# Windowed attention of the odd layer: values become the stationary operand, and the softmax sums are divided inside the transposes of the probabilities

## The chip, the cores and the metric

The kernel runs on one core of a Trainium2 chip. The metric is the device time of one execution in microseconds (us). The engines are named as the profile names them: PE is TensorE's matmuls and PEld its weight loads, DVE is VectorE, ACT is ScalarE, POOL is GpSimd, SP issues most of the DMAs.

## What is computed

The program is a two-layer backbone over 256 context tokens and 512 latent tokens of width 1024. The even layer mixes mLSTM heads with differential attention, the odd layer is sliding-window attention, and each layer ends in a large expert retrieval (PEER). The change touches only the odd layer's attention. It has 16 query heads of width 64 on 4 key-value heads; each block of 128 latent queries sees the 256 context keys and the latent blocks next to it, and one sink logit per head joins the softmax:

```python
def _sink_softmax(s, sink):
    sk = jnp.broadcast_to(sink[None, :, :, None, None], s.shape[:-1] + (1,))
    p = jax.nn.softmax(jnp.concatenate([s, sk], axis=-1), axis=-1)
    return p[..., :-1]
...
        p = _sink_softmax(jnp.concatenate([s_ctx, s_loc], axis=-1), sink).astype(vi.dtype)
        return (jnp.einsum('bhgqk,bkhd->bqhgd', p[..., :tc], vc)
                + jnp.einsum('bhgqk,bkhd->bqhgd', p[..., tc:], vi))
...
    yl = _window_attend(ql, kl, vl, kc, vc, sink) @ w_out
```

## The kernel before

The odd layer's attention works in 64 units. A unit is one head and one block `b` of 128 queries; units run over two passes `p` (blocks 0 and 1, then 2 and 3), in a pass over eight head pairs `j`, and for each pair over two blocks and the two heads `hf` of the pair. Four units share one query projection (`proj`, L251, tile `oqps`).

For one unit, `odd_front` (L1294) makes the scores in PSUM (`ops`: a one-column matmul for the sink, then matmuls over 256 context columns and over 256 or 384 latent columns, then the mask matmuls), takes the row minimum on DVE (`mx`, L1313; scores are kept negated) and the exponentials on ACT (`op`, L1315), whose sum over the row goes to a column of the tile `Z` (`oz`). `odd_back` (L1318) cuts the probabilities into chunks of 128 keys: 4 for the outer blocks 0 and 3, 5 for blocks 1 and 2, 288 over all units. PE transposes each chunk against the identity (`opt`, L1329), in two groups (2+2 or 3+2); ACT copies each group out of PSUM (`opT`, L1330). Then PE multiplies the transposed chunks, as stationary operand, with the values (`oo`, L1335), and ACT copies 64 columns of the result into the token-major tile `ys[b]` (`oy`, L1337).

After the last unit, DVE takes the reciprocal of `Z` (L1287) and multiplies each block's `ys[b]` by it (L1290); PE transposes each block in 8 pieces (`xpose`, L388, tile `xps`), ACT copies it to `xt` (L390), and `out_proj` (L836) multiplies `xt` with the output weights (L223, tile `ops`, the same name as the scores).

Two other streams share this stretch. The first is what is left of the expert gather of layer 0: 64 rows fetched by POOL and added up on DVE (`pacc<-uv`, L1036), after which latent block 3 can be normalized. The second is `mod_rows` (L323): 32 weight tiles `wraw` are read by DMA and added up on DVE (`macc`, L332 and L334) for layer 1's modulation rows. They share a ring of three `wraw` buffers with the weights of the projections.

The order of the instructions on each engine is fixed when the kernel is built, by a scheduler that weighs priorities and estimated times; on the chip each engine works through its own list and waits where it must. PSUM tiles of the kinds `opt`, `oo` and `rps` share two buffers, score tiles another two.

Of the kernel before, what the change touches and what calls it, by code (L numbers as in the profile page):

```python
# [9 lines left out]
F32 = mybir.dt.float32  # L10
# [3 lines left out]
AF = mybir.ActivationFunctionType  # L14
OP = mybir.AluOpType
AX = mybir.AxisListType

D = 1024
# [92 lines left out]
class Kern:  # L111
# [1071 lines left out]
    def odd(self, xs, tok_lat, late):  # L1183
        nc, a = self.nc, self.a
        wn = self.wk

        def norm_blocks(blocks, xt):
            old, self.wk = self.wk, wn
            self.norm_blocks(1, LAT, tok_lat, blocks, xt)
            self.wk = old  # L1190

        w_in = "od_w_in"
        xtc = self.xt_tiles(256)
        for b in range(2):
            self.xpose(xs[b], xtc, b)
        with self.tc.tile_pool(name="odk", bufs=1, reuse_waits="tile") as pk:
            KT = [[pk.tile([128, 768], F32R, name="okt%s%d" % (x, j)) for x in "hl"] for j in range(2)]
            V = pk.tile([128, 6, 256], F32, name="ov")

            snk = pk.tile([128, 16], BF16, name="snk")  # L1200
            rest = pk.tile([128, 16], F32, name="snr")
            part = pk.tile([128, 16], BF16, name="snp")
            nc.sync.dma_start(rest, a["od_sink"].broadcast_to([128, 16]))
            nc.gpsimd.memset(snk, 0.0)
            nc.vector.tensor_scalar(rest, rest, -1.0, None, op0=OP.mult)
            for r in range(3):
                nc.vector.tensor_copy(part, rest)
                nc.vector.scalar_tensor_tensor(snk, part, self.ident[:, r:r + 1], snk, op0=OP.mult, op1=OP.add)
                if r < 2:
                    nc.vector.tensor_tensor(rest, rest, part, op=OP.subtract)  # L1210
            bfc = pk.tile([128, 4, 128], BF16, name="bfc")
            for i, n in enumerate(("ident", "mf", "mb", "ones")):
                nc.vector.tensor_scalar(bfc[:, i, :], self.c(n), -1.0 if n in ("mf", "mb") else 1.0, None,
                                        op0=OP.mult)
            def keys(xt, c0, T, lat, skip=0):

                for j in range(2):
                    ps = self.pj([128, T], "okps")
                    self.projT(ps, self.wT(w_in, 1024 + 128 * j), xt, T, c0)
                    n = T - skip  # L1220
                    k = ps[:, skip:T]
                    if lat:
                        r = self.t2k([128, n], "okr")
                        self.rope(k, n, [(r, slice(0, 128))], c0 + skip)
                        k = r
                    hi, lo = (t[:, 256 * lat + c0 + skip:256 * lat + c0 + T] for t in KT[j])
                    nc.scalar.copy(hi, k)
                    nc.vector.tensor_tensor(lo, k, hi.bitcast(F32), op=OP.subtract)

            def values(xt, blocks, lat):  # L1230
                wv = [self.wN(w_in, 1280, h) for h in range(2)]
                for b in blocks:
                    ps = self.pj([128, 256], "vps")
                    self.projN(ps, wv, xt, b)
                    nc.scalar.copy(V[:, 2 * lat + b, :], ps)

            with self.later():
                late()
            with self.phase("okv"):
                keys(xtc, 0, 256, 0)  # L1240
                values(xtc, range(2), 0)
            xt = self.xt_tiles(512)
            norm_blocks(range(3), xt)
            with self.phase("okv"):
                keys(xt, 0, 384, 1)
                values(xt, range(3), 1)
            with self.phase("oat"):
                ys = [self.wk.tile([128, D], F32, name="oy%d" % b) for b in range(4)]
                Z = self.wk.tile([128, 4, 16], F32, name="oz")

                def proj(p, j):
                    ps = self.pj([128, 256], "oqps")
                    self.projT(ps, self.wT(w_in, 128 * j), xt, 256, 256 * p)
                    r = self.t2k([128, 256], "oqr")
                    self.rope(ps, 256, [(r, slice(0, 128))], 256 * p, -(64.0 ** -0.5))
                    t = [self.wk.tile([128, 2, 256], F32R, name="oq" + x, tag="oq" + x, bufs=2) for x in "hl"]
                    for n, ps in enumerate((slice(0, 64), slice(64, 128))):
                        hi, lo = t[0][ps, n, :], t[1][ps, n, :]
                        nc.scalar.copy(hi, r[ps, :])
                        nc.vector.tensor_tensor(lo, r[ps, :], hi.bitcast(F32), op=OP.subtract)  # L1260
                        for x in t:
                            nc.gpsimd.memset(x[ps, 1 - n, :].bitcast(F32), 0.0)
                    return t

                units = [(j, b, hf) for p in range(2) for j in range(8)
                         for b in (2 * p, 2 * p + 1) for hf in range(2)]
                qs = {(0, 0): proj(0, 0)}
                mods = self.mod_rows(1, [2, 4, 3, 5])

                def front(u):  # L1270
                    j, b, hf = u
                    p = b // 2
                    if MS == 0 and hf or MS == 1 and p == 1 or MS == 2 and (p == 1 or hf and j >= 4):
                        next(mods, None)
                    if b % 2 == 1 and hf == 0:
                        if (p, j) == (0, 7):
                            norm_blocks([3], xt)
                            keys(xt, 256, 256, 1, 128)
                            values(xt, [3], 1)
                        if (p, j) != (1, 7):  # L1280
                            nx = (p, j + 1) if j < 7 else (1, 0)
                            qs[nx] = proj(*nx)
                    return self.odd_front(j, b, hf, qs[p, j], KT[j // 4], snk, bfc, Z)

                self.pipe(units, front, lambda u, r: self.odd_back(*u, r, V, ys))
                xt = self.xt_tiles(512)
                nc.vector.reciprocal(Z, Z)  # L1287
                for b in range(4):
                    y = ys[b].rearrange("p (h d) -> p h d", h=16)
                    nc.vector.tensor_tensor(y, y, Z[:, b, :].unsqueeze(2).broadcast_to([128, 16, 64]), op=OP.mult)  # L1290
                    self.xpose(ys[b], xt, b)
        return xt

    def odd_front(self, j, b, hf, qp, kt, snk, bfc, Z):  # L1294
        nc, wk = self.nc, self.wk
        h = 8 * (j // 4) + 4 * hf + j % 4
        lo, hi = max(b - 1, 0), min(b + 1, 3)
        n = 128 * (hi - lo + 1)
# [4 lines left out]
        for c, d, m in ((0, 256, 256), (256 + 128 * lo, 512, n)):  # L1303
            for i, (x, y) in enumerate(((0, 0), (0, 1), (1, 0))):
                nc.tensor.matmul(S[:, d:d + m], q[x], kt[y][:, c:c + m], start=(i == 0),
                                 stop=(i == 2 and d == 256))
        masks = ([(0, 1)] if lo < b else []) + ([(n - 128, 2)] if hi > b else [])
        for i, (o, m) in enumerate(masks):
            nc.tensor.matmul(S[:, 512 + o:640 + o], bfc[:, 0, :], bfc[:, m, :], start=False,
                             stop=(i == len(masks) - 1))  # L1310
# [1 line left out]
        mx = wk.tile([128, 1], F32, name="mx", tag="mx", bufs=4)  # L1312
        nc.vector.tensor_reduce(mx, Sv, axis=AX.X, op=OP.min)  # L1313
        p = wk.tile([128, 641], F32, name="op", tag="op", bufs=3)
        nc.scalar.activation(p[:, 0:257 + n], Sv, AF.Exp, bias=mx, scale=-1.0, accum_out=Z[:, b, h:h + 1])  # L1315
        return p

    def odd_back(self, j, b, hf, p, V, ys):  # L1318
        nc, wk = self.nc, self.wk
        h = 8 * (j // 4) + 4 * hf + j % 4  # L1320
        lo, hi = max(b - 1, 0), min(b + 1, 3)
        kb = 2 + hi - lo + 1
        pT = wk.tile([128, kb, 128], F32, name="opT", tag="opT", bufs=2)
        i0 = 0
        for n in ((2, 2) if kb == 4 else (3, 2)):
            pt = self.po([128, n, 128], "opt")
            for i in range(n):
                c = 1 + 128 * (i0 + i)
                nc.tensor.transpose(pt[:, i, :], p[:, c:c + 128], self.ident)  # L1329
            nc.scalar.copy(pT[:, i0:i0 + n, :], pt)  # L1330
            i0 += n
        po = self.po([128, 128], "oo")
        for i in range(kb):
            vb = i if i < 2 else 2 + lo + i - 2
            nc.tensor.matmul(po, pT[:, i, :], V[:, vb, 128 * (j // 4):128 * (j // 4) + 128],  # L1335
                             start=(i == 0), stop=(i == kb - 1))
        nc.scalar.copy(ys[b][:, 64 * h:64 * h + 64], po[:, 64 * hf:64 * hf + 64])  # L1337


    def peer(self, l, xt, bb, gat, rows, done, late, put):  # L1340
# [134 lines left out]
def layout(i):  # L1475
# [26 lines left out]
        heads += [8 * (j // 4) + j % 4, 8 * (j // 4) + 4 + j % 4]  # L1502
    cols = np.concatenate([np.arange(64 * h, 64 * h + 64) for h in heads])
    ws["od_w_in"] = np.concatenate([w[:, cols], w[:, 1024:]], 1)
    ws["od_w_out"] = f("od_w_out")[0]
    o["od_sink"] = f("od_sink")
    for l in range(2):
        ws["pr_w_q%d" % l] = f("pr_w_q")[l]
# [8 lines left out]
    u = f("pr_u")  # L1517
# [30 lines left out]
```

## Time and profile before

| what | value |
|---|---|
| time, median of 3 runs | 4202.02 us (4199.56 to 4206.68) |
| the profiled execution | 4207.51 us, of which the span is 4205.7 us |
| PE / PEld busy | 3816.9 us (91%) / 3259.6 us (78%) |
| DVE busy | 3316.6 us (79%) |
| ACT / POOL busy | 1508.1 us (36%) / 2261.8 us (54%) |
| mean granted TensorE clock | 0.955 of full speed |

The span is the time from the first to the last instruction; the profiled execution's own time is 1.8 us longer. Busy shares are means over stages with different limits: the odd layer's attention fills about 290 us from 2490 us to 2782 us of the span, and it has to be read there.

### The profile page before, as it was taken

The numbers are of one execution on the slowest core, as the hardware profiler recorded it, in microseconds if no ns is written. First come the engines' busy times: TensorE is split into PE (matmuls) and PEld (weight loads), VectorE is DVE, ScalarE is ACT, GpSimd is POOL, SyncE is SP. The second block draws the span as 40 slices with busy tenths as digits, with TensorE's granted clock in tenths as the row PEclk, the third lists the DMA queues.
The fourth block names the chain that finished last, engine by engine and source line by source line (L and its number), as shares of the span: only waits on it lengthen the run. The fifth ranks groups of instructions, "written<-read, shape, count | busy, mean of one in ns | idle before, by whom it ended". The sixth has DMA issues, their size and how long they took to land.

```text
span 4205.7 us, 56328 instructions
## 1 busy us (share of the span) xinstructions
PE 3816.9 (91%) x19774; PEld 3259.6 (78%) x19780; DVE 3316.6 (79%) x5835; ACT 1508.1 (36%) x2746; POOL 2261.8 (54%) x1644
## 2 busy tenths in 40 slices
PE   8988776769888799999999889999989999999999
PEld 5776554547777699988999767777877899999987
DVE  4359888866998899989999987537875977777788
ACT  3322322312146333333333324332356333333333
POOL 1016777542454587877888563004531666666664
PEclk9999888879999999999999999999999999999999
DMA  5556898783449999999999995423346988787878
GB/s 192 172 200 209 308 322 307 253 287 121 149 161 398 367 332 334 332 324 333 346 339 331 341 333 194 158 85 111 111 160 235 346 279 285 275 290 273 282 268 313
DMA packets 389674, 1099.30 MB, mean 261 GB/s; under 512 B 32959, under 2 KB 140807, under 8 KB 383246
## 3 DMA queue, kind: packets, MB, share of 16 engines
q0 software_dynamic: 147456, 536.94, 35.2%
q1 hardware_dynamic: 232142, 497.95, 34.6%
q10 hardware_dynamic: 9792, 60.82, 3.5%
q8 instruction: 155, 2.54, 0.2%
q14 instruction: 129, 1.06, 0.1%
HBM read 1024.18 MB, written 71.40 MB: 260 GB/s over the span
## 4 chain that ended last, share of the span: by engine, by line
PE 58%; DVE 16%; DMA 11%; issue 8%; POOL 6%; ACT 2%; SPq 0%; ACTq 0%; POOLq 0%; DVEq 0%
PE dacc L1178 20%; PE dA L217 18%; POOL uv L1010 4%; DMA uv<-in_pr_u_dram,ix 3%; PE ops L223 3%; DMA uv<-in_pr_v_dram,ix 3%; PE pqps L217 2%; DVE junkv L1023 2%; PE gps L1108 2%; DMA draw<-in_uT_dram 1%; PE oo L1335 1%; DVE pacc L1036 1%; PE gds L1091 1%; PE modps L252 1%; PE oqps L210 1%
## 5 line engine op out<-in xcount | busy, mean ns | idle before, releaser
L1178 PE MATMUL dacc<-dhi,dw 128*128 128x512 f32 x3072 | 983.7, 390 | 3.4 <-ACT dw L1171 1.9
L1010 POOL DMA_INDIRECT uv<-in_pr_u_dram,ix x512 | 669.4, 1307 | 447.7 <-DVE pa L1023 316.0
L1010 POOL DMA_INDIRECT uv<-in_pr_v_dram,ix x512 | 680.0, 1328 | 408.0 <-DVE pacc L1036 281.9
L1023 DVE CUSTOM_DVE_ANT_0 junkv<-uv,x 128x1024 bf16<-128x1024 f32 x512 | 692.6, 1353 | 65.0 <-DMA uv<-in_pr_u_dram,ix 60.9
L1036 DVE SCALAR_TENSOR_TENSOR pacc<-uv,pw,pacc 128x1024 f32<-128x1024 f32 x508 | 701.5, 1381 | 39.3 <-DMA uv<-in_pr_v_dram,ix 35.4
L1178 PEld LDWEIGHTS dacc<-dhi,dw 128*128 128x128 f32 x3072 | 576.5, 188 | 119.5 <-ACT dw L1171 2.2
L1123 POOL TENSOR_TENSOR dlo<-draw,dhi 128x1024 fp32r<-128x1024 f32 x210 | 545.0, 2596 | 194.9 <-ACT dhi L1122 191.4
L1122 ACT CAST dhi<-draw 128x1024 fp32r<-128x1024 f32 x467 | 489.0, 1050 | 404.9 <-issue 179.5
L1178 PE MATMUL dacc<-dlo,dw 128*128 128x512 f32 x1536 | 601.6, 392 | 5.2 <-DVE dlo L1123 5.2
L1168 DVE TENSOR_TENSOR dz<-dz,dG 128x384 f32<-128x384 f32 x256 | 416.9, 1642 | 73.6 <-ACT dz L1138 71.8
L1171 ACT CAST dw<-dz 128x384 fp32r<-128x384 f32 x256 | 131.5, 514 | 721.2 <-PE dacc L1178 694.3
L1123 DVE TENSOR_TENSOR dlo<-draw,dhi 128x1024 fp32r<-128x1024 f32 x257 | 331.9, 1292 | 17.7 <-ACT dhi L1122 16.1
L217 PE MATMUL dA<-xth,dlo 128*128 128x384 f32 x1688 | 328.1, 335 | 19.0 <-POOL dlo L1123 19.0
L217 PE MATMUL dA<-xth,dhi 128*128 128x384 f32 x1688 | 334.6, 340 | 5.1 <-ACT dhi L1122 5.1
L1178 PEld LDWEIGHTS dacc<-dlo,dw 128*128 128x128 f32 x1536 | 288.2, 188 | 63.8 <-DVE dlo L1123 7.6
L217 PE MATMUL dA<-xtl,dhi 128*128 128x384 f32 x1688 | 326.9, 334 | 0.0
L217 PEld LDWEIGHTS dA<-xth,dhi 128*128 128x128 f32 x1688 | 305.7, 189 | 21.6 <-ACT dhi L1122 5.5
L217 PEld LDWEIGHTS dA<-xth,dlo 128*128 128x128 f32 x1688 | 296.5, 188 | 20.0 <-POOL dlo L1123 20.0
L217 PEld LDWEIGHTS dA<-xtl,dhi 128*128 128x128 f32 x1688 | 296.4, 188 | 0.0
L1172 DVE TENSOR_TENSOR dw<-dz,dw 128x384 fp32r<-128x384 f32 x256 | 154.4, 603 | 150.3 <-ACT dw L1171 150.3
L196 POOL TENSOR_TENSOR wlo<-wraw,whi 128x1024 fp32r<-128x1024 f32 x55 | 132.8, 2416 | 246.7 <-ACT whi L195 129.6
L1108 PEld LDWEIGHTS gps<-ghot 128*128 128x128 f32 x1536 | 205.0, 195 | 70.7 <-issue 39.0
(339 smaller groups left out, 6072.2 us busy)
## 6 DMA issues: line engine op xcount, KB each, us to landing
draw<-in_pr_v_dram SPq DMA_DIRECT2D x256, 512.0 KB
draw<-in_uT_dram SPq DMA_DIRECT2D x211, 512.0 KB
wraw<-in_wb_dram SPq DMA_DIRECT2D x150, 512.0 KB
gd<-gch ACTq DMA_DIRECT2D x48, 1024.0 KB
dG<-gd SPq DMA_DIRECT2D x30, 1536.0 KB
wraw<-in_mod_t_dram SPq DMA_DIRECT2D x48, 512.0 KB
wraw<-in_uT_dram SPq DMA_DIRECT2D x45, 512.0 KB
wraw<-in_mod_w_dram SPq DMA_DIRECT2D x32, 512.0 KB
```

What stands on the lines that cost most here:

```text
L196: eng.tensor_tensor(lo, raw, hi.bitcast(F32), op=OP.subtract)
L217: self.nc.tensor.matmul(ps, w[wi][:, k, :], x[xi][:, k, 0:T], start=(i == 0), stop=(i == 23))
L1010: nc.gpsimd.indirect_dma_start(out=t, out_offset=None, in_=a[table], in_offset=bass.IndirectOffsetOnAxis(ap=ix[:, c:c + 1], axis=0))
L1023: nc.vector.tensor_tensor_reduce(out=junk, in0=u, in1=x, op0=OP.mult, op1=OP.add, scale=1.0, scalar=0.0, accum_out=A[:, c:c + 1])
L1036: nc.vector.scalar_tensor_tensor(acc, v, W[:, c:c + 1], acc, op0=OP.mult, op1=OP.add)
L1108: nc.tensor.matmul(ps[0][:, t0 % 8 + t, :], h[0][:, t, :], h[1][:, t, :], start=True, stop=True)
L1122: nc.scalar.copy(hi, raw)
L1123: eng.tensor_tensor(lo, raw, hi.bitcast(F32), op=OP.subtract)
L1168: nc.vector.tensor_tensor(z3, z3, self.G[:, :, j % JG, :], op=OP.mult)
L1171: nc.scalar.copy(wh, z)
L1172: i = nc.vector.tensor_tensor(wl, z, wh.bitcast(F32), op=OP.subtract)
L1178: self.nc.tensor.matmul(acc[b][:, h, :], w[wi][:, 128 * b:128 * b + 128], v[vi][:, 512 * h:512 * h + 512], start=(j == 0 and i == 0), stop ...
```

## The change

The change turns the last product round: the values are now the stationary operand and the transposed probabilities the moving one, so `oo` comes out with the head's width on the partitions and the tokens along the row. ACT copies 64 partitions of 128 tokens straight into `yT` (tile `oy`, now allocated where the low parts of other transposed inputs lie), which is what the output projection reads. `ys`, the division at the end, the 32 transposes of `xpose` and their four copies are gone. The softmax sum must then be divided earlier: each unit takes the reciprocal of its own sum `z`, DVE multiplies the identity by it (`orz`, a 128x128 diagonal), and the transposes of the probabilities become ordinary f32 matmuls against this diagonal. The rows of the output weights are put in the order of the heads on the host.

```diff
@@ odd, phase "oat"
-                ys = [self.wk.tile([128, D], F32, name="oy%d" % b) for b in range(4)]
-                Z = self.wk.tile([128, 4, 16], F32, name="oz")
+                yT = self.px.tile([128, 8, 512], F32, name="oy", tag="xl")
...
-                    return self.odd_front(j, b, hf, qs[p, j], KT[j // 4], snk, bfc, Z)
-
-                self.pipe(units, front, lambda u, r: self.odd_back(*u, r, V, ys))
-                xt = self.xt_tiles(512)
-                nc.vector.reciprocal(Z, Z)
-                for b in range(4):
-                    y = ys[b].rearrange("p (h d) -> p h d", h=16)
-                    nc.vector.tensor_tensor(y, y, Z[:, b, :].unsqueeze(2).broadcast_to([128, 16, 64]), op=OP.mult)
-                    self.xpose(ys[b], xt, b)
+                    return self.odd_front(j, b, hf, qs[p, j], KT[j // 4], snk, bfc)
+
+                self.pipe(units, front, lambda u, r: self.odd_back(*u, r, V, yT))
+                xt = yT
         return xt
@@ odd_front
-        nc.scalar.activation(p[:, 0:257 + n], Sv, AF.Exp, bias=mx, scale=-1.0, accum_out=Z[:, b, h:h + 1])
-        return p
+        z = wk.tile([128, 1], F32, name="oz", tag="oz", bufs=4)
+        nc.scalar.activation(p[:, 0:257 + n], Sv, AF.Exp, bias=mx, scale=-1.0, accum_out=z)
+
+        nc.vector.reciprocal(z, z)
+        rz = wk.tile([128, 128], F32, name="orz", tag="orz", bufs=3)
+        nc.vector.tensor_scalar(rz, self.ident, z, None, op0=OP.mult)
+        return p, rz
@@ odd_back
-                nc.tensor.transpose(pt[:, i, :], p[:, c:c + 128], self.ident)
+                nc.tensor.matmul(pt[:, i, :], p[:, c:c + 128], rz, start=True, stop=True)
...
-            nc.tensor.matmul(po, pT[:, i, :], V[:, vb, 128 * (j // 4):128 * (j // 4) + 128],
+            nc.tensor.matmul(po, V[:, vb, 128 * (j // 4):128 * (j // 4) + 128], pT[:, i, :],
                              start=(i == 0), stop=(i == kb - 1))
-        nc.scalar.copy(ys[b][:, 64 * h:64 * h + 64], po[:, 64 * hf:64 * hf + 64])
+        rows = slice(64 * hf, 64 * hf + 64)
+        nc.scalar.copy(yT[rows, j, 128 * b:128 * b + 128], po[rows, :])
@@ layout, on the host
-    ws["od_w_out"] = f("od_w_out")[0]
+    ws["od_w_out"] = f("od_w_out")[0][cols]
```

The first place is the end of the attention on PE. Before, between the last units and the output projection (`oo` are value products, `opt` transposes of probabilities, `xps` transposes of finished blocks, `ops<-wraw,xt` the output projection):

```order
L388 MATMUL xps<-cst,oy_19361 128x128 x8
L1335 MATMUL oo<-ov,opT 128x128 x2
L388 MATMUL xps<-cst,oy_19362 128x128 x8
L223 MATMUL ops<-wraw,xt 128x256 x5
L1335 MATMUL oo<-ov,opT 128x128 x2
L1329 MATMUL opt<-cst,op 128x128 x2
L223 MATMUL ops<-wraw,xt 128x256 x10
L1329 MATMUL opt<-cst,op 128x128 x2
L1335 MATMUL oo<-ov,opT 128x128 x2
L223 MATMUL ops<-wraw,xt 128x256
L1335 MATMUL oo<-ov,opT 128x128 x2
L388 MATMUL xps<-cst,oy_19363 128x128 x8
```

In the changed kernel, the same place up to the output projection (`ops<-wraw,oy`):

```order
L1329 MATMUL opt<-orz,op 128x128 x5
L1335 MATMUL oo<-opT,ov 128x128 x5
L1329 MATMUL opt<-orz,op 128x128 x5
L1335 MATMUL oo<-opT,ov 128x128 x5
L1329 MATMUL opt<-orz,op 128x128 x4
L1335 MATMUL oo<-opT,ov 128x128 x4
L1329 MATMUL opt<-orz,op 128x128 x4
L1335 MATMUL oo<-opT,ov 128x128 x4
L223 MATMUL ops<-wraw,oy 128x256 x112
L388 MATMUL xps<-cst,xn 128x128 x32
```

The groups of `xps` (three of the four show here) are gone, and the output projection, of which 16 matmuls stood between the last units, now begins after the last of them.

The second place is DVE in the stretch where the expert gather is still being added up (`pacc`); before, for the second group of four units:

```order
L1313 TENSOR_REDUCE mx<-ops 128x1 x2
L1036 SCALAR_TENSOR_TENSOR pacc<-uv,pw,pacc 128x1024
L334 SCALAR_TENSOR_TENSOR macc<-wraw,sc,macc 128x1024
L1036 SCALAR_TENSOR_TENSOR pacc<-uv,pw,pacc 128x1024
L1313 TENSOR_REDUCE mx<-ops 128x1
L334 SCALAR_TENSOR_TENSOR macc<-wraw,sc,macc 128x1024
L1313 TENSOR_REDUCE mx<-ops 128x1
L1036 SCALAR_TENSOR_TENSOR pacc<-uv,pw,pacc 128x1024
L725 TENSOR_TENSOR rt_19600<-rps,cst 128x256
L726 TENSOR_TENSOR rraw<-rraw,cst 128x256
```

In the changed kernel, for the same four units:

```order
L1307 TENSOR_REDUCE mx<-ops 128x1
L1312 RECIPROCAL oz<-oz 128x1
L334 SCALAR_TENSOR_TENSOR macc<-wraw,sc,macc 128x1024
L1314 TENSOR_SCALAR orz<-cst,oz 128x128
L1307 TENSOR_REDUCE mx<-ops 128x1
L1036 SCALAR_TENSOR_TENSOR pacc<-uv,pw,pacc 128x1024
L1312 RECIPROCAL oz<-oz 128x1
L1307 TENSOR_REDUCE mx<-ops 128x1
L1036 SCALAR_TENSOR_TENSOR pacc<-uv,pw,pacc 128x1024
L334 SCALAR_TENSOR_TENSOR macc<-wraw,sc,macc 128x1024
L1314 TENSOR_SCALAR orz<-cst,oz 128x128
L1312 RECIPROCAL oz<-oz 128x1
```

Each unit adds one RECIPROCAL (`oz`) and one TENSOR_SCALAR (`orz`), set between the sums of the gather and of the modulation rows.

The third place is PE in the second pass, where nothing but attention is left. Before, between the scores of two blocks:

```order
L1335 MATMUL oo<-ov,opT 128x128 x4
L1329 MATMUL opt<-cst,op 128x128 x2
L1302 LDWEIGHTS bfc
L1302 MATMUL ops<-snk,bfc 128x1
L1305 MATMUL ops<-okth_18937,oqh 128x256
L1305 MATMUL ops<-oktl_18938,oqh 128x256
L1305 MATMUL ops<-okth_18937,oql 128x256
L1305 MATMUL ops<-okth_18937,oqh 128x256
L1305 MATMUL ops<-oktl_18938,oqh 128x256
L1305 MATMUL ops<-okth_18937,oql 128x256
```

In the changed kernel:

```order
L1329 MATMUL opt<-orz,op 128x128 x2
L1335 MATMUL oo<-opT,ov 128x128 x2
L1296 LDWEIGHTS bfc
L1296 MATMUL ops<-snk,bfc 128x1
L1299 MATMUL ops<-okth_18937,oqh 128x256
L1299 MATMUL ops<-oktl_18938,oqh 128x256
L1299 MATMUL ops<-okth_18937,oql 128x256
L1299 MATMUL ops<-okth_18937,oqh 128x256
L1299 MATMUL ops<-oktl_18938,oqh 128x256
L1299 MATMUL ops<-okth_18937,oql 128x256
L1303 LDWEIGHTS bfc
L1303 MATMUL ops<-bfc 128x128
```

The value product of the unit before is cut in two, and the first transposes of the next unit (`opt`) moved behind one more group of scores.

## Rows read from the trace of the kernel before

**Rows 1.** Busy time by stretch: microseconds of the span, then busy (instructions) per engine.
```profile
core 0: us, PE busy (x) PEld busy (x) DVE busy (x) ACT busy (x) POOL busy (x), PEclk, DMA share, GB/s
2498.50:2578.00 79.50, 73.26 (x512) 61.56 (x511) 76.65 (x90) 39.13 (x114) 42.72 (x51) 1.00 0.86 309
2578.00:2722.00 144.00, 132.15 (x838) 106.87 (x836) 77.68 (x119) 58.93 (x169) 12.05 (x31) 0.96 0.42 136
2722.00:2761.00 39.00, 37.98 (x288) 32.95 (x288) 15.08 (x28) 23.24 (x68) 1.96 (x7) 1.00 0.08 28
```

**Rows 2.** Transposes and value products by tile: count, duration ns min/median/max, first and last start.
```profile
L1329 PE MATMUL opt<-cst,op x288: 272/273/331, 2497.2 to 2777.8; 128*128 128x128 f32 x144
L1335 PE MATMUL oo<-ov,opT x576: 272/275/377, 2499.9 to 2779.1; 128*128 128x128 f32 x192
```

**Rows 3.** The chain that ended last, end of the attention: start us, us, what.
```profile
2758.18 0.95 PE oo L1335 x8
...
2761.06 0.07 PE ops L1309
...
2767.41 0.87 PE xps L388 x8
...
2770.70 2.16 PE ops L223 x10
...
2773.52 4.32 PE ops L223 x20
...
2778.51 0.43 PE ops L223 x2
...
2779.66 1.24 DVE oy L1290
...
2780.94 1.09 PE xps L388 x8
2782.04 7.99 PE ops L223 x37
```

**Rows 4.** The transposes alone (L1329) by stretch: PE busy, PEld busy, clock, DMA.
```profile
2498.50:2578.00 79.50, 16.78 (x88) 9.98 (x88) 1.00 0.86 309
2578.00:2722.00 144.00, 22.86 (x122) 13.90 (x122) 0.96 0.42 136
2722.00:2761.00 39.00, 10.37 (x55) 6.03 (x56) 1.00 0.08 28
2761.00:2782.10 21.10, 3.69 (x20) 2.27 (x20) 1.00 0.08 23
```

**Rows 5.** The row minima alone (L1313), one per unit: DVE busy (instructions).
```profile
2498.50:2578.00 79.50, 14.79 (x20) 1.00 0.86 309
```

**Rows 6.** Small DVE operations, groups by shape: busy us, mean ns | idle before.
```profile
L788 DVE RECIPROCAL darz<-daz 128x2 f32<-128x2 f32 x24 | 3.9, 164 | 18.3 <-ACT dap L785 18.3
...
L1213 DVE TENSOR_SCALAR bfc<-cst 128x128 bf16<-128x128 f32 x4 | 0.6, 220 | 0.0
L728 DVE TENSOR_TENSOR okr<-rraw,rt 128x128 f32<-128x128 f32 x2 | 0.6, 280 | 0.0
```

**Rows 7.** The chain that ended last, one group of four units later on.
```profile
2731.93 1.12 PE ops L1305 x8
...
2738.53 0.34 PE opt L1329 x3
...
2738.94 0.49 ACT opT L1330
...
2743.93 1.12 PE ops L1305 x8
```

**Rows 8.** Waits from 2578 to 2722 us: total us, times, longest.
```profile
DVE macc L334 <- DMA wraw<-in_mod_w_dram: 29.0, 12, 13.5
...
PE oqps L210 <- DMA wraw<-in_wb_dram: 4.7, 3, 2.9
```

**Rows 9.** The chain that ended last, two query projections of 16 passes.
```profile
2504.76 3.46 PE oqps L210 x16
...
2670.12 6.62 PE oqps L210 x16
```

More of the change, by code (lines that the diff above doesn't have):

```diff
@@ L1282, in front, with odd_front @@
                             qs[nx] = proj(*nx)
-                    return self.odd_front(j, b, hf, qs[p, j], KT[j // 4], snk, bfc, Z)
-                self.pipe(units, front, lambda u, r: self.odd_back(*u, r, V, ys))
-                xt = self.xt_tiles(512)
-                nc.vector.reciprocal(Z, Z)
-                for b in range(4):
-                    y = ys[b].rearrange("p (h d) -> p h d", h=16)
-                    nc.vector.tensor_tensor(y, y, Z[:, b, :].unsqueeze(2).broadcast_to([128, 16, 64]), op=OP.mult)
-                    self.xpose(ys[b], xt, b)
+                    return self.odd_front(j, b, hf, qs[p, j], KT[j // 4], snk, bfc)
+                self.pipe(units, front, lambda u, r: self.odd_back(*u, r, V, yT))
+                xt = yT
         return xt
-    def odd_front(self, j, b, hf, qp, kt, snk, bfc, Z):
+    def odd_front(self, j, b, hf, qp, kt, snk, bfc):
         nc, wk = self.nc, self.wk
@@ L1314, in odd_front, with odd_back @@
         p = wk.tile([128, 641], F32, name="op", tag="op", bufs=3)
-        nc.scalar.activation(p[:, 0:257 + n], Sv, AF.Exp, bias=mx, scale=-1.0, accum_out=Z[:, b, h:h + 1])
-        return p
-    def odd_back(self, j, b, hf, p, V, ys):
+        z = wk.tile([128, 1], F32, name="oz", tag="oz", bufs=4)
[4 more added lines that the diff above has]
+        return p, rz
+    def odd_back(self, j, b, hf, r, V, yT):
         nc, wk = self.nc, self.wk
-        h = 8 * (j // 4) + 4 * hf + j % 4
+        p, rz = r
         lo, hi = max(b - 1, 0), min(b + 1, 3)
```

## Prediction

> **What bounds the kernel now.** I first looked at busy time by stretch, because the mean shares of the page hide that the attention of the odd layer has three different limits [rows 1]. From 2498.5 to 2578 us DVE is the limit: it is busy 76.65 of 79.5 us, since it adds up the last rows of the expert gather beside the attention. PE is busy 73.26 us there, but much of that is the tails of single matmuls. How much room PE has is seen better from the length of a unit: 20 row minima, one per unit, lie in this stretch [rows 5], so a unit takes 79.5 / 20 = 4.0 us. Later, when nothing but attention is left, the same point of the program comes round every four units at 2731.93 and 2743.93 us in the chain [rows 7], so a unit then takes 12.0 / 4 = 3.0 us. PE thus has about 1.0 us to spare in each unit of the first stretch. From 2578 to 2722 us PE is busy 132.15 of 144 us and runs at 0.96 of its clock; the 11.9 us of gaps are mixed, and 4.7 us of them are waits for projection weights [rows 1, 8]. From 2722 to 2761 us PE is full, 37.98 of 39 us. Then I read the chain through the end of the attention [rows 3]: it lies on PE nearly everywhere, and once the last score is done it is still 20.9 us (2761.13 to 2782.03) until the last block stands transposed.
>
> **What a transposed chunk costs.** The count is the first thing to see [rows 2]: the 288 transposes are 288 PE instructions, but the 288 value products, which are f32 matmuls of the same 128x128x128 shape, are 576. An f32 matmul goes through PE twice, a transpose once. The durations (273 and 275 ns) are nearly equal and say nothing, since both are mostly latency; what counts is how fast they follow each other. In the chain, eight transposes take 0.87 us, 0.109 us each, and eight passes of value products take 0.95 us, 0.119 us each, so 0.238 us for one product [rows 3]. The changed chunk is an f32 matmul of that very shape, with the probabilities stationary and a diagonal moving, so I price it as a value product. The extra is 0.238 - 0.109 = 0.13 us by this row, and 0.109 us if the second pass costs as much as a transpose; I take 0.12 us. Over 288 chunks this is 34.6 us more work on PE.
>
> [...]
>
> The turned value product has the same shape and also a new stationary operand each time, so I cost it at nothing. Its copy grows from 128x64 to 64x128 elements on ACT, which is busy 23.24 of 39 us even where PE is full [rows 1]; nothing waits long for it.
>
> **First stretch, 88 chunks, 20 units** [rows 4, 5]. PE gets 88 x 0.12 = 10.6 us, 0.53 us a unit, within its 1.0 us to spare. DVE is full, and gets a reciprocal and a product with the identity for each unit. A reciprocal of two columns took 0.164 us; a TENSOR_SCALAR of 128x128 took 0.22 us with 16-bit output, and a two-operand operation of that size in f32 0.28 us [rows 6]. I take 0.16 + 0.22 = 0.38 us a unit, 7.5 us for 20. The bounds are 6 us, since following operations overlap a little, and 9 us by the 0.28 us. Behind these two stand the gather's sums, as the second place of the change shows. **+7.5 us.**
>
> **Middle stretch, 122 chunks, 30 units** [rows 4]. PE gets 122 x 0.12 = 14.6 us. Some is covered: in units of five chunks the second group of two is transposed while ACT copies the first group (0.49 us, after which PE goes on) [rows 7]; two chunks times 0.12 us in about 15 such units is 3.6 us. Some of the 4.7 us of waits for weights shrinks when PE comes later; I take 3 us. DVE is busy only 77.68 of 144 us and carries its share. **+8 us**, with 0 (all in the 11.9 us of gaps) and 14.6 us as bounds.
>
> **Full stretch, 55 chunks** [rows 4]. 55 x 0.12 = 6.6 us, less six places where two chunks lie under the copy (1.4 us). The sum is now needed before the first transpose, and so the reciprocal and the product (0.38 us) and ACT's reading of the sum stand in the unit's chain. I cost that at nothing, because the third place of the change shows a group of scores put ahead of the first transpose. If that cover were gone, it would be 0.4 us or a little more in each of 12 units, 5 us. **+5.2 us.**
>
> **The end** [rows 3, 4]. Of the 20.9 us, 2.16 + 4.32 + 0.43 = 6.9 us are output projection done early, which is needed anyway. The other 14.0 us are 20 chunks, 22 value products, 32 block transposes and the waits between them, the last one for the division (1.24 us) and its neighbours. In the changed kernel 20 chunks and 22 products at 0.23 us are 9.7 us, and two waits for copies of 0.2 us make it 10.1 us. Nothing fills these waits, since the output projection stands behind the last unit, but it can then run through. **-3.9 us.** The projection's blocks have long been complete by then.
>
> The sum is 7.5 + 8 + 5.2 - 3.9 = +16.8 us, about **+17 us**. Against the profiled execution (4207.51 us; the span is 4205.7 us) this gives 4224.5 us. That execution is 5.5 us above the median of the runs, so against the median of 4202.0 us I predict **4219 us**.
>
> **Rivals.** *The new wait on DVE* (slower still). In the middle stretch DVE sat 29.0 us over 12 waits for modulation weights [rows 8]. DVE works in order, and the transposes now wait for `orz`, which can stand behind such a sum. One wait of 13.5 us fell where little attention was ready; if the other 11 (15.5 us) held up PE in full, the time is 4219 + 15 = 4234 us. Against it: the row minima stood behind the same sums already.
>
> *Absorbed* (no change). If PE's gaps in the middle take all of the 14.6 us, the sum is 7.5 + 0 + 5.2 - 3.9 = +9 us; with DVE at its lower bound of 6 us and the copies covering 3 us more in the full stretch, +4 us: 4206 us. This needs 14.6 us to fit in 11.9 us of gaps that are partly real waits.
>
> [...]
>
> [...]
>
> **How the numbers follow.** A difference under 0.2% (8.4 us) can't be told from no change. My forecast, +9 to +28 us, has 0.60; the DVE wait 0.17; absorbed 0.16; faster 0.05; four passes 0.02. So slower is 0.60 + 0.17 + 0.02 = 0.79, same 0.16, faster 0.05. The range goes from 4205 us, near the absorbed case, to 4237 us, above the DVE wait; outside lie the faster case, the four passes and a little of the two edges.
>
> **What would show it.** `opt` must appear as 576 PE instructions instead of 288; if it stays at 288, the price is wrong. Four units late in the stretch should take about 13.6 us instead of 12.0. The stretch that ends with the gather should be about 7 us longer with DVE full. From the last score to the output projection's unbroken run it should be about 10 us. If PE waits for `orz` in the waits of the middle stretch, the DVE rival is right; if the chain there moves to the modulation weights without getting longer, the absorbed one is.

## The result and the profile after

The changed kernel takes 4228.16 us (median of 11 runs, 4214.82 to 4237.76) against 4206.68 us before (median of 11 runs): the ratio is 1.0051, with a 95% interval from 1.004 to 1.0061. It is 21.5 us slower; 17 us were forecast, with a range up to 4237 us.

The page of the changed kernel, span and busy times:

```profile
span 4227.5 us, 56998 instructions
...
PE 3847.9 (91%) x20030; PEld 3295.6 (78%) x20036; DVE 3331.3 (79%) x5958; ACT 1508.3 (36%) x2742; POOL 2254.2 (53%) x1644
```

PE is busy 31 us more than before, DVE 15 us more. The tiles of the change, as a count and the smallest, median and largest duration in ns:

```profile
L1329 PE MATMUL opt<-orz,op x576: 270/275/583, 2495.9 to 2801.1; 128*128 128x128 f32 x192
...
L1312 DVE RECIPROCAL oz<-oz x64: 141/156/165, 2493.2 to 2795.0; 128x1 f32<-128x1 f32 x64
L1314 DVE TENSOR_SCALAR orz<-cst,oz x64: 265/285/2119, 2493.4 to 2795.3; 128x128 f32<-128x128 f32 x64
```

The 288 chunks, 288 instructions in [rows 2], are now 576 on PE. The reciprocal took the 0.16 us that I had put in, the diagonal 0.285 us where I had put in 0.22 us.

To see where the time went, cut both traces at the same points of the program: where the query projection at 2504.6 us (2501.4 us after) begins, where the keys of block 3 begin (`okps`, the first product on PE that reads that block's transposes, 2604.2 us before), where the last query projection begins, and where the output projection ends. The busy times of these three parts, before:

```profile
core 0: us, PE busy (x) PEld busy (x) DVE busy (x) ACT busy (x) POOL busy (x), PEclk, DMA share, GB/s
2504.60:2604.20 99.60, 91.98 (x661) 78.29 (x660) 85.14 (x103) 53.77 (x154) 45.32 (x58) 1.00 0.65 234
2604.20:2723.80 119.60, 110.02 (x665) 87.61 (x664) 64.13 (x100) 42.56 (x124) 8.04 (x24) 0.96 0.49 159
2723.80:2830.40 106.60, 103.59 (x629) 90.77 (x628) 37.57 (x66) 34.88 (x95) 1.23 (x4) 1.00 0.22 80
```

And of the changed kernel:

```profile
2501.40:2616.10 114.70, 107.78 (x786) 96.81 (x786) 93.14 (x156) 56.07 (x156) 48.58 (x58) 0.97 0.58 205
2616.10:2741.40 125.30, 117.59 (x757) 98.78 (x756) 70.52 (x141) 44.22 (x124) 7.32 (x24) 0.97 0.46 152
2741.40:2853.50 112.10, 108.64 (x666) 96.65 (x666) 37.49 (x87) 31.74 (x90) 1.22 (x4) 1.00 0.21 76
```

The three parts got 15.1, 5.7 and 5.5 us longer, 26.3 us together. The first cut lies 3.2 us earlier in this execution, and what follows the last cut is 1.3 us shorter, which leaves the 21.8 us between the two spans. The end of the attention, in the chain that ended last:

```profile
2791.03 0.07 PE ops L1303
2791.10 0.50 PE opt L1329 x4
...
2793.54 0.49 ACT opT L1330
...
2794.07 1.38 PE oo L1335 x10
...
2800.36 1.06 PE opt L1329 x8
2801.42 1.17 PE oo L1335 x8
2802.60 5.20 PE ops L223 x24
...
2807.81 7.43 DMA wraw<-in_wb_dram
...
2815.28 2.86 PE ops L223 x12
```

From the last score (2791.10) to the output projection it is 11.5 us, where the like of it had been 14.0 us [rows 3]. (Not all of the projection stands behind the last unit, as I had read it: 32 of its 256 passes come earlier, 16 each at 2749.46 and 2766.77 us. The other 224 follow the last unit's work, as before.) But then something stands there that was not there before: the projection stops for a DMA of its own weights. PE's waits over the whole stretch name it, and one more new one:

```profile
PE opt L1329 <- DVE orz L1314: 3.8, 2, 3.1
...
PE ops L223 <- DMA wraw<-in_wb_dram: 2.3, 1, 2.3
```

Ahead of these weights in SP's queue of loads stand those of the rows `oh`, to which the projection's result is added. Before:

```profile
2779.41 1.74 SPq L844 DMA_DIRECT2D oh<-h  x4
...
2787.25 27.95 SPq L187 DMA_DIRECT2D wraw<-in_wb_dram  x5
```

And after:

```profile
2802.63 1.74 SPq L844 DMA_DIRECT2D oh<-h  x4
...
2807.81 30.55 SPq L187 DMA_DIRECT2D wraw<-in_wb_dram  x5
```

The weights are issued 5.2 us after the projection's long run begins (2782.04 us [rows 3] and 2802.60 us) in both. But the rows were issued 2.6 us ahead of that run before, and start together with it now.

### The profile page after: what moved, and what is told of

Same layout as the page of the kernel before. It is cut to its first block, busy times and chain, and to the rows that moved or that the text cites. A ratio compares the mean times of both kernels' runs of the same rounds, so it can differ in the third digit from the quotient of the medians.

```text
span 4227.5 us, 56998 instructions
## 1 busy us (share of the span) xinstructions
PE 3847.9 (91%) x20030; PEld 3295.6 (78%) x20036; DVE 3331.3 (79%) x5958; ACT 1508.3 (36%) x2742; POOL 2254.2 (53%) x1644
## 4 chain that ended last, share of the span: by engine, by line
PE 54%; DVE 16%; DMA 13%; issue 8%; POOL 6%; ACT 2%; SPq 0%; ACTq 0%; POOLq 0%; DVEq 0%
PE dacc L1178 19%; PE dA L217 17%; DMA uv<-in_pr_u_dram,ix 5%; POOL uv L1010 4%; PE ops L223 3%; DMA uv<-in_pr_v_dram,ix 3%; PE pqps L217 2%; DMA draw<-in_uT_dram 2%; PE gps L1108 2%; DVE junkv L1023 2%; DVE pacc L1036 1%; PE oo L1335 1%; PE gds L1091 1%; PE opt L1329 1%; PE modps L252 1%
## 5 line engine op out<-in xcount | busy, mean ns | idle before, releaser
L1123 DVE TENSOR_TENSOR dlo<-draw,dhi 128x1024 fp32r<-128x1024 f32 x257 | 334.4, 1302 | 21.5 <-ACT dhi L1122 19.2
```

What stands on the lines that cost most here:

```text
L1123: eng.tensor_tensor(lo, raw, hi.bitcast(F32), op=OP.subtract)
```

## The experiments

The ratio is to the kernel before on the same chip, with its 95% interval; the difference in us is that ratio on 4205 us.

| run | PE passes per chunk | diagonal on DVE | rest as | ratio (95%) | us |
|---|---|---|---|---|---|
| the change | 2 | yes | after | 1.0051 (1.0040 to 1.0061) | +21 |
| before_two_pass | 2 | no | before | 1.0051 (1.0039 to 1.0064) | +21 |
| two_pass_no_diag | 2 | no | after | 1.0058 (1.0045 to 1.0071) | +24 |
| one_pass_with_diag | 1 | yes | after | 1.0010 (1.0001 to 1.0019) | +4 |
| one_pass_no_diag | 1 | no | after | 1.0006 (0.9997 to 1.0016) | +3 |
| before_plus_diag | 1 | yes | before | 0.9994 (0.9985 to 1.0004) | -3 |

Two theories stood against each other: that the second PE pass of each chunk is the cost, and that the small DVE operations and the waits for them are.

**One pass, with the diagonal.** The diagonal is made and not used.

```diff
-                nc.tensor.matmul(pt[:, i, :], p[:, c:c + 128], rz, start=True, stop=True)
+                nc.tensor.transpose(pt[:, i, :], p[:, c:c + 128], self.ident)
```

> The changed kernel with the chunks transposed against the identity again (one PE pass); the reciprocal and the diagonal are still made on DVE but nothing reads them, so the division is left out. Theory PE (the second pass of 288 f32 matmuls is the cost): the 8 + 5.2 + 2.3 us of the middle, the full stretch and the end go away, DVE's 7.5 us stays in the first stretch and the shorter end gives 6.2 us, so about +1 us against the kernel before, within 4 us. Theory DVE (the 128 small DVE operations and the waits for them are the cost): nearly the full +21 us stays. In between, some +10 us, if the transposes' wait for the diagonal is what costs, since that wait is gone here too.

Measured: +4 us. Some 17 of the 21 us go with the second pass.

**Two passes, no diagonal.**

```diff
-        nc.vector.reciprocal(z, z)
-        rz = wk.tile([128, 128], F32, name="orz", tag="orz", bufs=3)
-        nc.vector.tensor_scalar(rz, self.ident, z, None, op0=OP.mult)
+        rz = None
...
-                nc.tensor.matmul(pt[:, i, :], p[:, c:c + 128], rz, start=True, stop=True)
+                nc.tensor.matmul(pt[:, i, :], p[:, c:c + 128], self.ident, start=True, stop=True)
```

> The changed kernel with f32 matmuls against the plain identity, no reciprocal and no diagonal; the division is left out. Theory PE: 8 + 5.2 us of extra passes and 3.9 us less at the end, +9 us against the kernel before, plus up to 3 us for the weights that the output projection now waits for. Theory DVE: -4 us, since only the shorter end is left.

Measured: +24 us, not below the change itself. Taking all 128 DVE operations away brings nothing back, so the theory that DVE is the cost has fallen; and the theory of the passes had been sized too small, since it gave +9 to +12 us.

**One pass, no diagonal.** Both edits together: the turned values and the transposed output alone.

> Turned values and transposed output alone: one-pass transposes, no reciprocal, no diagonal; the division is left out. Both theories: only the shorter end is left, -6 us by my sum (14.0 us of the end less 20 x 0.11 + 22 x 0.24 + waits), or -4 us if the wait for the output weights of 2.3 us stays. If it is at zero or above, the turned product or its copy costs something that I priced at nothing.

Measured: +3 us, not to be told from 0, and not the -6 us that both theories gave. The turned product is not the reason: ten of its passes take 1.38 us in the chain after (2794.07 us above), as ten of the old product's do before:

```profile
2763.48 1.38 PE oo L1335 x10
```

The three parts of the trace of this run:

```profile
2504.40:2604.50 100.10, 92.04 (x660) 78.20 (x659) 85.20 (x103) 55.09 (x154) 45.92 (x58) 1.00 0.65 234
2604.50:2720.80 116.30, 107.29 (x664) 85.68 (x663) 64.10 (x100) 43.75 (x124) 8.02 (x24) 0.99 0.50 164
2720.80:2828.20 107.40, 102.38 (x597) 87.43 (x596) 32.10 (x61) 31.92 (x91) 1.22 (x4) 1.00 0.22 79
```

The third part has 32 PE instructions fewer (the block transposes) and is no shorter, 107.4 against 106.6 us. What PE waits for from 2776 to 2830 us:

```profile
PE ops L223 <- DMA wraw<-in_wb_dram: 2.2, 1, 2.2
PE ops L223 <- DVE ot L852: 0.7, 1, 0.7
```

**The kernel before with two passes.** The output is the same.

```diff
-                nc.tensor.transpose(pt[:, i, :], p[:, c:c + 128], self.ident)
+                nc.tensor.matmul(pt[:, i, :], p[:, c:c + 128], self.ident, start=True, stop=True)
```

> The kernel before with its 288 transposes written as f32 matmuls against the identity, all else as it was. Theory PE: +8 + 5.2 + 2.3 = +15.5 us, and up to +20 us if the first stretch does not hide its 10.6 us wholly. Theory DVE: 0 us, since no DVE operation is added. [...]

Measured: +21 us, the whole of the change's loss by this one line. Its three parts:

```profile
2499.80:2612.70 112.90, 107.31 (x786) 97.38 (x786) 83.90 (x104) 54.79 (x156) 45.43 (x59) 0.97 0.59 207
2612.70:2734.80 122.10, 115.43 (x748) 96.87 (x747) 63.34 (x99) 41.94 (x121) 8.04 (x24) 0.99 0.47 156
2734.80:2850.10 115.30, 112.52 (x708) 100.98 (x707) 37.55 (x66) 35.87 (x98) 1.22 (x4) 1.00 0.20 74
```

They are 13.3, 2.5 and 8.7 us longer. (The first cut lies 4.8 us earlier here and what follows is 1.7 us longer, so of these 24.5 us 21.4 us are left between the spans.) Before, 117, 93 and 71 chunks lie in them, which at 0.114 us each (below) are 13.3, 10.6 and 8.1 us. The third part gives the second pass back in full.

The other two can't be read so directly, because the granted clock differs. In the first part it is 0.97 instead of 1.00, by my estimate worth up to 0.03 x 112.9 = 3.4 us; in the middle it is 0.99 instead of 0.96, worth up to 0.03 x 119.6 = 3.6 us the other way. Two one-pass kernels with 0.99 in the middle take 116.3 us (above) and 115.8 us (below, with diagonals) there, 6 us less than the 122.1 us here. That leaves some 10 to 13 us to the passes in the first part, and about 6 us in the middle.

Four units late in the attention took 12.0 us before [rows 7]. Here, in the chain, they take 13.74 us, so 1.74 us of their 18 x 0.114 = 2.05 us arrive:

```profile
2758.97 1.12 PE ops L1305 x8
...
2772.71 1.12 PE ops L1305 x8
```

One thing this line of code changes besides the passes: the scheduler builds another list from it. From the first cut until the gather's block is normalized, 16 row minima are taken instead of 20, and at the end 16, 12 and 4 passes of the projection stand between the last units instead of 10, 20 and 2. No run holds the order fixed; that more passes cost more (four passes, below) speaks for the passes.

**Two passes in one half only.** Blocks 0 and 1 (the first 32 units), or blocks 2 and 3:

```diff
-                nc.tensor.transpose(pt[:, i, :], p[:, c:c + 128], self.ident)
+                if b < 2:
+                    nc.tensor.matmul(pt[:, i, :], p[:, c:c + 128], self.ident, start=True, stop=True)
+                else:
+                    nc.tensor.transpose(pt[:, i, :], p[:, c:c + 128], self.ident)
```

> The kernel before with f32 matmuls in place of transposes only for blocks 0 and 1 (the first 32 units, 144 chunks, 17.3 us of PE work by 0.12 us each). As predicted (the first stretch hides PE's second pass behind DVE, 88 of these chunks): only what lies behind the gather counts, +3 to +4 us against the kernel before. Rival (a unit's chain through PE, DVE and ACT sets the pace there, so that PE time lands in it although DVE is 96% busy): +9 to +13 us, about half of the +22 us of all chunks.

> The kernel before with f32 matmuls only for blocks 2 and 3 (the last 32 units, 144 chunks). As predicted: +12 us (5 of the middle, 5 of the full stretch, 2 at the end). Rival as for the first half: +9 to +13 us here too, and the two halves add up to +22 us.

Measured: 1.0016 (1.0002 to 1.0031), +7 us, and 1.0025 (1.0015 to 1.0035), +10.5 us. The intervals are wide; the first half lies between the two expectations. Its trace shows why. The three parts:

```profile
2502.60:2613.80 111.20, 107.54 (x785) 97.35 (x784) 83.75 (x103) 54.58 (x156) 45.23 (x59) 0.97 0.60 212
2613.80:2728.10 114.30, 107.30 (x682) 86.95 (x682) 63.51 (x99) 42.27 (x124) 8.02 (x24) 1.00 0.50 167
2728.10:2834.80 106.70, 103.70 (x629) 90.92 (x628) 37.60 (x66) 34.90 (x95) 1.22 (x4) 1.00 0.22 80
```

The first part is 11.6 us longer, of which the clock of 0.97 instead of 1.00 explains at most 0.03 x 111.2 = 3.3 us by the same estimate, so PE's passes are not hidden there. The middle part, where only the last few units of the first half have the second pass, is 5.3 us shorter than before: its clock reads 1.00 instead of 0.96, and PE's wait for weights, 4.7 us in [rows 8], is 3.1 us there.

**The diagonal in the kernel before**, made and read by nobody:

```diff
+        z = wk.tile([128, 1], F32, name="ozr", tag="ozr", bufs=4)
+        nc.vector.reciprocal(z, Z[:, b, h:h + 1])
+        rz = wk.tile([128, 128], F32, name="orz", tag="orz", bufs=3)
+        nc.vector.tensor_scalar(rz, self.ident, z, None, op0=OP.mult)
```

> The kernel before with one reciprocal and one 128x128 diagonal more per unit on DVE, which nothing reads; the output is unchanged. As predicted (DVE is full in the first stretch): +7.5 us. Rival (DVE has room between the links of the units' chain, so that 64 x 0.44 us of small operations fit in): 0 to +3 us.

Measured: 0.9994 (0.9985 to 1.0004), no cost. The trace shows that the price was right and still did not count. Its first two parts:

```profile
2502.60:2603.80 101.20, 92.91 (x661) 79.31 (x660) 90.71 (x156) 53.83 (x154) 43.40 (x58) 0.98 0.66 231
2603.80:2719.60 115.80, 106.48 (x664) 85.37 (x663) 70.86 (x142) 42.45 (x124) 8.02 (x24) 0.99 0.51 165
```

(The second line is the middle part.) DVE has 5.6 us more to do in the first part, which is 1.6 us longer at a clock of 0.98 instead of 1.00; and the gather's block is normalized (`xn`) at 2587.43 us here:

```profile
2587.43 1.28 DVE L379 SCALAR_TENSOR_TENSOR xn<-hr,rstd,mr 128x1024 f32<-128x1024 f32 x1 [0.43 <-ACT rstd L370]
```

and before at 2580.91 us:

```profile
2580.91 1.27 DVE L379 SCALAR_TENSOR_TENSOR xn<-hr,rstd,mr 128x1024 f32<-128x1024 f32 x1
```

POOL adds the last term to the block (2.4 us, until 2591.22 us here and 2584.67 us before), and then PE transposes it for the keys. These transposes begin at 2600.87 us here, and before at

```profile
2601.28 1.04 PE L388 MATMUL xps<-cst,xn 128*128 128x128 f32 x8
```

PE stands idle in front of them in neither trace; in both, the chunks that it transposes just ahead of them begin 0.33 us earlier. The 6.5 us were taken out of the 16.6 us in which the block lay ready.

**The residual rows early.** In the changed kernel, the rows `oh` that the output projection adds to are allocated in a pool that is free during the attention, so their loads need not wait for its end:

```diff
-        hs = [self.wk.tile([128, D], F32, name="oh%d" % b) for b in range(nb)]
+        hs = [(hw or self.wk).tile([128, D], F32, name="oh%d" % b) for b in range(nb)]
```

> The changed kernel with the four residual rows of the output projection (oh) in a pool that is free during the attention, so that their four loads no longer wait for the end of the attention and no longer stand ahead of the projection's weights. Theory: the 2.3 us in which PE waits for weights goes away, and the DVE sums after it start earlier: -2 to -4 us against the changed kernel, +17 to +20 us against the kernel before. Rival: the weights wait for their buffer alone, and nothing changes (+21 us).

> Turned values and transposed output with one-pass transposes, no reciprocal, no diagonal (the division is left out), and the residual rows oh loaded during the attention. Theory (the shorter end was eaten by waits for these rows and for the weights behind them, 2.9 us): -3 us against the same kernel without early rows, so about 0 to -3 us against the kernel before. If it stays at +2 us or more, the shorter end is lost elsewhere.

Measured: 1.0058 (1.0045 to 1.0071) for the changed kernel, no gain; and 0.9998 (0.9988 to 1.0007) for the one with one pass and no diagonal, -1 us against the kernel before and 3.4 us less than without early rows, at the edge of what the intervals can tell. In both traces the wait for weights is gone; the third part of the first kernel is 110.3 us instead of 112.1 us. The third part of the second kernel:

```profile
2727.80:2832.50 104.70, 102.06 (x597) 87.65 (x596) 32.11 (x61) 31.91 (x91) 1.22 (x4) 1.00 0.18 61
```

It is 104.7 us instead of 107.4 us, and PE's waits for DMA in it have gone:

```profile
PE ops L223 <- DVE ot L852: 0.5, 1, 0.5
PE oo L1333 <- ACT opT L1328: 0.3, 2, 0.2
```

So the mechanism is shown in the trace; in the time it shows at most faintly.

**Four passes.** Each chunk is made twice:

```diff
-                nc.tensor.transpose(pt[:, i, :], p[:, c:c + 128], self.ident)
+                for _ in range(2):
+                    nc.tensor.matmul(pt[:, i, :], p[:, c:c + 128], self.ident, start=True, stop=True)
```

> The kernel before with each chunk made twice by an f32 matmul against the identity (the second overwrites the first with the same values): 4 PE passes for each chunk instead of one. If what the first extra pass lost in waits is used up by then, two more passes cost 288 x 0.24 = 69 us in full, about +90 us against the kernel before (22 for the first). If waits hide a fixed share (22 of 34.6 us arrive, 64%), +66 us.

Measured: 1.0172 (1.0159 to 1.0186), +72 us, near the 66 us of a fixed share and well below 90 us. In its chain, eight passes of chunks follow each other in 0.89 us, 0.112 us each:

```profile
2773.42 0.89 PE opt L1330 x8
```

A chunk of two passes is thus 0.223 us against 0.109 us [rows 3], 0.114 us more; 288 of them are 33 us, of which 21 arrive, and three more passes are 97 us, of which 72 arrive. I can't say from this alone where the rest is hidden.

**Two ways to keep the good part.** The changed kernel with one-pass transposes and the division in the probabilities, and the kernel before with the division in ACT's copy:

```diff
-        rz = wk.tile([128, 128], F32, name="orz", tag="orz", bufs=3)
-        nc.vector.tensor_scalar(rz, self.ident, z, None, op0=OP.mult)
+        nc.vector.tensor_scalar(p[:, 1:257 + n], p[:, 1:257 + n], z, None, op0=OP.mult)
+        rz = None
```

> Turned values and transposed output, one-pass transposes, and the division made on DVE in the probabilities themselves before they are transposed (one TENSOR_SCALAR of 128 x 512 or 640 instead of the diagonal); the output is the reference's. By the PE theory and DVE's room: +2 to +6 us against the kernel before, some 16 to 20 us faster than the changed kernel. If DVE counts after all: +10 us or more.

```diff
-        nc.scalar.copy(ys[b][:, 64 * h:64 * h + 64], po[:, 64 * hf:64 * hf + 64])
+        nc.scalar.activation(ys[b][:, 64 * h:64 * h + 64], po[:, 64 * hf:64 * hf + 64], AF.Identity, scale=z)
```

> The kernel before with the division made by ACT while it copies each unit's result out of PSUM (the reciprocal of the unit's own sum as ACT's scale), so that the division at the end and its wait go away; one small reciprocal per unit is added on DVE. Theory: the end gets 2 to 3 us shorter and nothing else changes, -2 to -3 us, hardly to be told from 0. Rival: the scaled copy waits for the reciprocal behind DVE's long sums, +2 us or more.

Measured: 1.0012 (1.0000 to 1.0023) and 1.0010 (1.0000 to 1.0020), +5 and +4 us. The first does all that the change does and is some 16 us faster than it, but neither beats the kernel before. In the second, the wait for the division is gone from the end, and the output projection waits for its weights instead:

```profile
PE ops L223 <- DMA wraw<-in_wb_dram: 1.6, 1, 1.6
```

## Why the prediction was right, and where its steps were not

The direction and most of the size were right, for the main reason given: the f32 matmul with a diagonal takes two passes where the transpose took one (576 PE instructions for the 288 chunks, where there had been 288). 0.114 us a chunk was measured where 0.12 us was taken: 0.223 us for a chunk of two passes is 2.05 times the 0.109 us of a transpose. But that 17 us came out near 21 us is in part luck. Put on the three parts, my terms are +9.4, +6.1 and +1.3 us; the changed kernel's parts are 15.1, 5.7 and 5.5 us longer, and 4.5 us came off ahead of and behind them, for which I had no term.

**First stretch: wrong in its reason.** I wrote that PE's 10.6 us lie within its 1.0 us to spare per unit and that DVE's 7.5 us count. It is the other way round. The diagonals did move the end of the gather by about the predicted amount (6.5 us), but PE had no use for the block for another 16.6 us, and the kernel before with diagonals is no slower. The second pass landed there, 10 to 13 us for 117 chunks. The sign that I had named, a longer stretch with DVE full, would have misled: until the gather's block is normalized the changed kernel takes 85.0 us instead of 76.3 us, but DVE is busy 75.7 us of them (89%) where it had been 72.7 us (95%). A unit took 4.0 us there not because PE had 1.0 us over: the same time passes if PE, DVE and ACT take turns in one unit's chain, and then PE's time adds to it. That this chain is the reason is only argued; that PE's passes land there, and that DVE's diagonals cost nothing where nothing reads them, is shown. Where PE reads them, one wait is new (see the rivals).

**Middle: about right.** By my rates, the second part should have gained 93/122 of 8 us, 6.1 us; it gained 5.7 us in the changed kernel, and with the passes alone about 6 us against kernels with the like clock. PE's waits for projection weights shrank, as said, from 4.7 us to 2.9 us.

**Full stretch and end: the passes right, the gain at the end lost.** With the old end, the third part gained 8.7 us, where 5.2 + 2.3 us were worked out; four units took 13.74 us, where I had said 13.6 us. The shorter end was to give back 6.2 us of that. It did shorten the way to the output projection (14.0 us to 11.5 us, where 10.1 us were expected), but the projection then waited 2.3 us for weights. Their load stands on SP's queue behind those of the rows `oh`, which wait for the attention's memory (before those rows SP's queue stood 56.5 us, the last value product being what it waited for); before, while PE waited for the division and did the last transposes, the rows had 2.6 us of lead. I had not asked what the projection would wait for next. With rows loaded early the wait goes, and the third part with one pass is 1.9 us shorter than before instead of 6.2 us; its end takes 10.5 us from the last score (2773.36 to 2783.86 us), where I had 14.0 - 6.2 = 7.8 us. In the last four units there, the products begin 1.11, 1.12, 0.91 and 0.89 us after the chunks of their unit, 4.03 us together, where 18 chunks of 0.109 us are 1.96 us; the other 2.07 us are, by my reading, waits for ACT's copies, for which I had put in 0.4 us. Another 1.3 us go between the last query projection and the last score (38.7 us instead of 37.3 us, without the 32 early passes of the output projection).

**The rivals.** PE did wait for the diagonal, 3.8 us in two waits, in place of the 15 us of that rival, and the same kernel without a diagonal is no faster. The long wait is the rival's mechanism at another place, in the first part: DVE stood 4.57 us for a row of the gather, and a diagonal stood behind that sum.

```profile
2570.35 1.28 DVE L1036 SCALAR_TENSOR_TENSOR pacc<-uv,pw,pacc 128x1024 f32<-128x1024 f32 x1 [4.57 <-DMA uv<-in_pr_v_dram,ix]
...
2571.98 1.20 PE L1329 MATMUL opt<-orz,op 128*128 128x128 f32 x4 [3.12 <-DVE orz L1314]
```

No run shows what the chances of the faster case (0.05) and of four passes (0.02) rest on. What the runs showed: the mean granted clock is 0.956 after and 0.955 before, over the three parts it went from 1.00, 0.96 and 1.00 to 0.97, 0.97 and 1.00, and a chunk takes two passes.

## What to carry to other kernels

A transpose and a matmul against a diagonal look the same in the code and even in the median duration (273 ns and 275 ns here), but the f32 matmul took two passes, 576 instructions for 288 chunks; count the PE instructions of a tile before arithmetic is folded into a transpose. DVE was 96% busy here and still not the bound: 5.6 us more of work on it cost nothing (0.9994), since PE took up its block 16.6 us after it lay ready. So look for the first reader of a result, and how long that is idle or elsewhere. When a tail is cut away, look at what used it as lead time, above all the loads queued behind the memory that the tail frees: four loads had 2.6 us of lead here, and a wait of 2.3 us came in its place.

## What the runs showed of the hardware

One of the 64 diagonals took 2.12 us instead of 0.285 us. It began while POOL added to the gather's block:

```profile
2588.42 2.12 DVE L1314 TENSOR_SCALAR orz<-cst,oz 128x128 f32<-128x128 f32 x1
```

```profile
2587.85 2.37 POOL L381 TENSOR_TENSOR xn<-xn,mr 128x1024 f32<-128x1024 f32 x1 [18.30 <-issue]
```

It ended 0.32 us after POOL's addition. PE did not wait for it by the trace. The same stands in other traces. With diagonals in the kernel before, the one that began beside POOL's addition (2588.85 to 2591.22 us) took 0.94 us, and ended 0.08 us after it; in the kernel before, a product of 128x256 that takes 0.42 us otherwise took 2.52 us, and ended 0.29 us after the addition:

```profile
2590.36 0.94 DVE L1319 TENSOR_SCALAR orz<-cst,ozr 128x128 f32<-128x128 f32 x1
```

```profile
2582.32 2.35 POOL L381 TENSOR_TENSOR xn<-xn,mr 128x1024 f32<-128x1024 f32 x1 [14.56 <-PE rps L723]
...
2582.44 2.52 DVE L726 TENSOR_TENSOR rraw<-rraw,cst 128x256 f32<-128x256 f32 x1
```

Not every DVE operation was held so: two row minima, which read PSUM, took 1.28 us together beside the same addition in the kernel with diagonals, as such a pair takes in the kernel before (2510.28 us):

```profile
2588.63 1.28 DVE L1313 TENSOR_REDUCE mx<-ops 128x1 f32<-128x513 f32 x2
```

```profile
2510.28 1.28 DVE L1313 TENSOR_REDUCE mx<-ops 128x1 f32<-128x513 f32 x2
```

No run isolates what the operations that were held have in common.

DVE operations that followed each other overlapped a little, as I had it for the bound of 6 us: two of 0.42 us start 0.34 us apart in the kernel before.

```profile
2502.80 0.42 DVE L725 TENSOR_TENSOR rt<-rps,cst 128x256 f32<-128x256 f32 x1
2503.14 0.42 DVE L726 TENSOR_TENSOR rraw<-rraw,cst 128x256 f32<-128x256 f32 x1
```
